# Strided attention scores that read ordered copies of q and k, made by Pool for each item

## The chip, the cores and the metric

The kernel runs on one core of one Trainium2 chip. The metric is the device time of one execution in microseconds; of several runs the median is taken. The core has five engines, each with an instruction list of its own that it takes in order: TensorE (PE; its weight loads are shown as PEld), VectorE (DVE), ScalarE (ACT), GpSimd (POOL) and SyncE (SP, which issues DMAs). They meet through semaphores.

## The reference

One layer of a hybrid decoder for a prompt of 2048 positions (and a small sample group of 8 x 4 rows), width 1024. What matters here is the attention of the prompt: 8 heads of 64 channels, each with three branches of dilated sliding windows, merged by the sums of their softmaxes:

```python
BRANCHES = ((128, 1), (512, 4), (2048, 16))      # window, dilation
def _dilated_prompt(q, k, v, bias_hj, d, nj):
    L = S // d
    ...
    s = jnp.einsum('bnqrhc,bnkrhc->bnrhqk', qb, kc).astype(jnp.float32)
    s = s * (HEAD_DIM ** -0.5) + bias[None, None, None]
    s = jnp.where(valid[None, :, None, None], s, NEG_INF)
    lse = jax.nn.logsumexp(s, axis=-1)
    p = jnp.exp(s - lse[..., None])
    o = jnp.einsum('bnrhqk,bnkrhc->bnqrhc', p.astype(vc.dtype), vc)
```

With dilation 16 a position sees only positions with the same residue modulo 16: each of the 16 residues is a causal attention of its own over 128 positions. Before the attention stand a normalisation and the input projection, behind it the output projection, a feed-forward network and a last normalisation.

## The kernel before

**Stages.** The input projection takes about the first 600 us, the attention the time from about 610 to 975 us, and output projection and feed-forward network the rest. The order on each engine is written out by hand: a planner (class `Plan`, lines 45 to 62) collects calls as (step, phase, function), and runs them step by step, within a step in the order of the phases "early", "exp", "low", "scores", "turn", "mid", "values", "out", "misc", "store". What a function issues goes to the ends of the engines' lists at that moment. Nothing holds an engine to its step: it goes on as soon as its next instruction has what it waits for.

**Attention items.** For one head, q and k lie in SBUF as [128, 2048] tiles with the positions along the row (load_head, L815). q comes as a rounded high part twice over ("qh") and a low part ("ql"), k as high and low part one above the other, so that one product with qh and one with ql make scores of full precision. A head has 16 band items (branches 1 and 2: 128 queries against up to 640 keys) and 4 strided items (branch 3: four residues each). The list OTHER (L1082) puts the strided items of a head at steps 2, 7, 12 and 17 of 20; head 0 has a list of its own (FIRST, strided items at 8, 11, 14 and 16 of 20), and so has head 7 (LAST: at 1, 3, 5 and 7 of 20).

**One strided item**, placed at step x (L1147 on):
- step x, "scores": strided_scores (L921). For each of four residues two products of 128x128 on TensorE. Stationary operand and moving operand are read straight from the head's tiles with a step of 16 elements, which is 64 bytes.
- step x + 1, "scores": strided_bias (L929). DVE adds the bias (L932) and takes the row minima (L934), Pool subtracts them (L935).
- steps x + 3 to x + 5: exp on ACT (L938), row sums on DVE (L942), four transposes on TensorE (L947), rounding on ACT (L950), low parts on DVE (L896).
- from step x + 6: strided_values (L953). Eight products of 128x128 (L958, L959), whose operands lie packed; then strided_out on ACT (L966), which writes its result with a step of 16 elements.

**Pool in this stage** has only the subtractions of L935 and the merges of the head before (merge, L1031): for each of four chunks three operations of 128x512 (L1036, L1038, L1040), one a step, at steps 11 to 22 behind that head's end, so that the last three stand in the first steps of the head after; they wait for factors that come by DMA. In the "scores" phase of a step a subtraction stands ahead of the merge of that step, which is in phase "store".

Scores land in PSUM tiles "ps_s", of which there are two (L79). A band item's scores (L859), transposes (L887) and values (L910) fill the rest of TensorE's list.

Of the kernel before, what the change touches and what calls it, by code (L numbers as in the profile page):

```python
# [11 lines left out]
F32R = mybir.dt.float32r  # L12
# [7 lines left out]
P = 128  # L20
T = 2048
NT = T // P
# [20 lines left out]
class Plan:  # L43
# [8 lines left out]
    def at(self, step, phase, fn, *args):  # L52
        self.events.append((step, self.PHASES.index(phase), self.n, fn, args))
        self.n += 1
# [10 lines left out]
def hymba_step(ctx: ExitStack, tc: tile.TileContext, A: dict, O: dict):  # L65
    nc = tc.nc
    sync, act, dve, pool, pe = nc.sync, nc.scalar, nc.vector, nc.gpsimd, nc.tensor
# [11 lines left out]
    def ps_s():  # L79
        return psum_s.tile([P, 2, 512], F32, name="ps_s", tag="s", bufs=2)  # L80
# [79 lines left out]
    at = plan.at  # L160
# [493 lines left out]
    for n in range(len(first) + 4):  # L654
        if n >= 4:
            (w_split if first[n - 4][0] == "w" else x_half_split)(*first[n - 4][1:])
        if n < len(first):
            if first[n][0] == "w":
                k = first[n][1]
# [39 lines left out]
    for half in range(2):  # L699
        for ki, kind in enumerate(ORDER[half]):  # L700
            for gi, tiles in enumerate(GROUPS):
                start = ((half * 5 + ki) * 3 + gi) * 8
                for k in range(KD):
                    if start == 0:

                        for j in range(3):
                            n = 3 * k + j
# [99 lines left out]
    heads, loads, sts, fs, obs, o3s = {}, {}, {}, {}, {}, {}  # L807
# [106 lines left out]
    def band_out(it):  # L914
# [3 lines left out]
        dst = obs[h][:, G * 512:(G + 1) * 512]  # L918
        act.activation(dst, it["grp"]["o"], AF.Copy)

    def strided_scores(it):  # L921
        d, st, r4 = it["d"], it["st"], it["n"]
        it["s"] = s = ps_s()[:, 0, :]
        for a in range(4):
            qs = bass.ds(r4 * 4 + a, P, step=NT)
            pe.matmul(s[:, a * P:(a + 1) * P], d["qh"][:, qs], d["k"][:, qs], start=True, stop=False)
            pe.matmul(s[:, a * P:(a + 1) * P], d["ql"][:, qs], d["k"][:, qs], start=False, stop=True)

    def strided_bias(it):  # L929
        d, st, r4, s = it["d"], it["st"], it["n"], it["s"]  # L930
# [155 lines left out]
    for h in range(H):  # L1086
        r4 = 0
# [31 lines left out]
    for h in range(H):  # L1119
# [4 lines left out]
        if end:  # L1124

            x = s0 - NI
# [21 lines left out]
    for i, it in enumerate(items):  # L1148
        x, h, n = B0 + i, it["h"], it["n"]

        at(x, "scores", scores, it)
        at(x + 1, "scores", bias, it)
        if it["kind"] == "s":
            at(x + 3, "exp", strided_exp, it)
            at(x + 4, "low", strided_sum, it)
            at(x + 4, "turn", strided_turn, it)
            at(x + 5, "mid", low_parts, it)
            v = min(y for y in range(x + 6, x + 14) if y not in taken)
            taken.add(v)
            at(v, "values", strided_values, it)  # L1160
            at(v + 1, "early", strided_out, it)
            continue
        at(x + 2, "exp", band_exp, it)
        at(x + 3, "turn", band_turn, it)
        at(x + 4, "low", low_parts, it)
        if n % 4 == 3:
            for part in range(3):
                at(x + 4 + part, "values", band_values, it, part)
            at(x + 7, "early", band_out, it)
# [9 lines left out]
    ap_ = left.enter_context(tc.tile_pool(name="attn", bufs=2, reuse_waits="tile"))  # L1179
# [525 lines left out]
    h = H - 1  # L1705
# [321 lines left out]
```

## Time and profile before

| what | value |
|---|---|
| median of 3 runs | 2704.91 us (2699.18 to 2713.04) |
| profiled execution | 2700.58 us, its span 2698.8 us |
| TensorE busy | 2554.9 us (95% of the span) |
| DVE, ACT, Pool busy | 1421.3, 1246.3, 1312.4 us |
| granted TensorE clock, mean | 0.966 |
| attention, 580 to 950 us: TensorE, DVE, ACT, Pool busy of 370 us | 339.9, 266.7, 255.0, 141.1 us |

A row of a group reads: line, engine, operation, result<-operands by the program's names, shape, count, then busy us, mean ns of one, and the idle time of the engine ahead of it with what ended that. A row of a timeline reads: start in us from the span's start, duration in us, engine, line, operation, count, and in brackets how long the engine sat idle before and on whom it waited. Matmuls are pipelined: one that starts every 0.11 us may be shown with 0.28 us each, so a pace is read from the starts of the weight loads.

### The profile page before, as it was taken

The page shows a single profiled execution, that of the slowest core. Times are in us where ns is not written, and L with a number is a line of the kernel's source. Part 1 is how long each engine was busy: PE and PEld are TensorE (multiplying, and loading weights), DVE is VectorE, ACT ScalarE, POOL GpSimd, SP SyncE. Part 2 cuts the span into 40 slices and gives each one's busy share as a digit, 9 for nine tenths or more (in the row PEclk, how much of TensorE's full clock was granted, in tenths as well). Part 3 has the DMA queues.
Part 4 walks back from the last instruction along what each step waited for, and adds up shares of the span by engine and source line. Part 5 has one row for each costly group of instructions (what it writes and reads, how often), then busy time and mean ns, then how long its engine had stood idle before and what let it go on. Part 6 is the DMA issues. An engine that isn't in the chain of part 4 may idle for free. (4 is left out here: it accounts for less than half of the span.)

```text
span 2698.8 us, 38876 instructions
## 1 busy us (share of the span) xinstructions
PE 2554.9 (95%) x13578; PEld 2253.8 (84%) x13578; DVE 1421.3 (53%) x2884; ACT 1246.3 (46%) x2649; POOL 1312.4 (49%) x960
## 2 busy tenths in 40 slices
PE   8998899998999978999999999999999998999997
PEld 6777677677888866999998987899999987999996
DVE  3268784436887864444434455344444455444445
ACT  5414344446777645645455444423232335433333
POOL 1036653221445353767676743536353533666663
PEclk9999899998999989899999999899999999899998
DMA  8765844686576565436455465436354553455553
GB/s 244 218 201 157 283 137 134 187 273 201 160 239 181 155 177 175 136 126 199 153 181 166 162 188 162 159 122 214 138 198 153 183 163 125 166 201 202 203 195 117
DMA packets 314679, 481.05 MB, mean 178 GB/s; under 512 B 26967, under 2 KB 179720, under 8 KB 308596
## 3 DMA queue, kind: packets, MB, share of 16 engines
q1 hardware_dynamic: 300100, 455.89, 52.1%
q10 hardware_dynamic: 14384, 22.68, 3.2%
q8 instruction: 108, 1.77, 0.3%
q14 instruction: 87, 0.71, 0.1%
HBM read 382.76 MB, written 165.84 MB: 203 GB/s over the span
## 5 line engine op out<-in xcount | busy, mean ns | idle before, releaser
L1472 POOL TENSOR_TENSOR op<-fr,op 128x512 fp32r<-128x512 f32 x385 | 489.0, 1299 | 318.3 <-ACT op L1468 281.1
L1529 PE MATMUL ps_m<-xh,op 128*128 128x384 f32 (+4 forms) x1932 | 629.6, 326 | 8.5 <-ACT xh L1406 5.3
L1530 PE MATMUL ps_m<-xl,op 128*128 128x384 f32 (+4 forms) x1932 | 627.8, 325 | 7.0 <-DVE xl L1409 7.0
L1531 PE MATMUL ps_m<-xh,op 128*128 128x384 f32 (+4 forms) x1932 | 627.6, 325 | 0.0
L1602 PE MATMUL ps_o<-dw,hw 128*128 128x512 f32 x2040 | 484.4, 392 | 8.8 <-DVE acc L1604 8.8
L1602 PEld LDWEIGHTS ps_o<-dw,hw 128*128 128x128 f32 x2040 | 379.6, 188 | 91.5 <-DVE acc L1604 15.9
L1529 PEld LDWEIGHTS ps_m<-xh,op 128*128 128x128 f32 x1932 | 377.6, 195 | 13.7 <-ACT xh L1406 5.9
L1530 PEld LDWEIGHTS ps_m<-xl,op 128*128 128x128 f32 x1932 | 377.8, 196 | 11.7 <-DVE xl L1409 7.7
L1531 PEld LDWEIGHTS ps_m<-xh,op 128*128 128x128 f32 x1932 | 377.3, 195 | 0.0
L1604 DVE TENSOR_TENSOR acc<-acc,ps_o 128x512 f32<-128x512 f32 (+1 forms) x362 | 247.0, 687 | 213.7 <-PE ps_o L1602 213.6
L1569 ACT ACTIVATE ps_t<-zn 128x384 f32<-128x384 f32 (+1 forms) x126 | 58.3, 463 | 481.1 <-DVE zn L1552 372.8
L1468 ACT ACTIVATE op<-fr 128x512 fp32r<-128x512 f32 x396 | 235.7, 622 | 19.0 <-DMA fr<-ab_d 13.7
L137 POOL TENSOR_TENSOR dw<-fd,dw 128x1024 fp32r<-128x1024 f32 x66 | 158.7, 2404 | 122.9 <-ACT dw L134 122.7
L317 PE MATMUL ps_s<-wh,xh 128*128 128x512 f32 x480 | 197.7, 412 | 6.7 <-ACT xh L134 6.7
L318 PE MATMUL ps_s<-wl,xh 128*128 128x512 f32 x480 | 192.2, 401 | 0.0
L319 PE MATMUL ps_s<-wh,xl 128*128 128x512 f32 x480 | 191.4, 399 | 0.0
L1472 POOL TENSOR_TENSOR op<-pair,op 128x512 fp32r<-128x512 f32 x63 | 81.3, 1299 | 116.1 <-ACT op L1468 116.1
L1579 ACT ACTIVATE hw<-ps_t 128x384 fp32r<-128x384 f32 (+1 forms) x126 | 56.1, 453 | 176.6 <-DVE ps_t L1575 175.6
L317 PEld LDWEIGHTS ps_s<-wh,xh 128*128 128x128 f32 x480 | 92.8, 193 | 36.5 <-issue 8.3
L935 POOL TENSOR_TENSOR e<-e,st 128x512 f32<-128x512 f32 x32 | 33.3, 1042 | 173.5 <-DVE st L934 118.1
L319 PEld LDWEIGHTS ps_s<-wh,xl 128*128 128x128 f32 x480 | 92.7, 193 | 20.6 <-DVE xl L137 0.2
L318 PEld LDWEIGHTS ps_s<-wl,xh 128*128 128x128 f32 x480 | 93.0, 194 | 18.4 <-DVE wl L225 1.1
(457 smaller groups left out, 4912.1 us busy)
## 6 DMA issues: line engine op xcount, KB each, us to landing
fr<-ab_d SPq DMA_DIRECT2D x308, 256.0 KB
fd<-in_w_down_dram SPq DMA_DIRECT2D x66, 512.0 KB
out_ks_dram<-in_cache_k_dram SPq DMA_DIRECT2D x56, 512.0 KB
out_vs_dram<-in_cache_v_dram SPq DMA_DIRECT2D x56, 512.0 KB
ab_d<-fr SPq DMA_DIRECT2D x88, 256.0 KB
raw<-in_w_in_dram SPq DMA_DIRECT2D x72, 256.0 KB
qk_d<-pair SPq DMA_DIRECT2D x64, 256.0 KB
ab_d<-pair SPq DMA_DIRECT2D x63, 256.0 KB
```

The lines of the kernel that those rows point to most:

```text
L137: (eng_lo or pool).tensor_sub(lo, src, hi.bitcast(F32))
L317: pe.matmul(o[j], xh[:, k, :], wh, start=(k == 0), stop=False)
L318: pe.matmul(o[j], xh[:, k, :], wl, start=False, stop=False)
L319: pe.matmul(o[j], xl[:, k, :], wh, start=False, stop=(k == KD - 1))
L1468: act.activation(ops[f, j][0], ab[f][j], AF.Copy)
L1472: (pool if f or j in POOL_LOW else dve).tensor_sub(lo_, ab[f][j], hi.bitcast(F32))
L1529: pe.matmul(out, wh[:, ks], xh[:, :, k], start=(k == 0), stop=False)
L1530: pe.matmul(out, wh[:, ks], xl[:, :, k], start=False, stop=False)
L1531: pe.matmul(out, wl[:, ks], xh[:, :, k], start=False, stop=(k == 3))
L1569: act.activation(g, c, AF.Silu)
L1602: pe.matmul(ps[0:nr], l_, r_[:, cs], start=(z == 0 and y == 0), stop=(z == FC - 1 and y == len(pairs) - 1))
L1604: dve.tensor_add(B.acc[i][0:nr, cs], B.acc[i][0:nr, cs], ps[0:nr])
```

## The change

A new function, strided_order, makes for each strided item a tile "sq" with three parts: k, qh and ql of that item's four residues, each residue's 128 positions packed. Pool makes it by three tensor_copy instructions, each of 128 x 4 x 128 elements, which read with a step of 16 elements and write packed. strided_scores reads its operands from that tile. There are two such tiles. The copies of an item at step x are put into the plan at step x - 2, phase "out". The products, their number, shapes and order stay the same, and so do all instructions of the other engines.

```diff
+    def strided_order(h, r4):
+
+        d = heads[h]
+        d["sq", r4] = t_ = ap_.tile([P, 3, 4, P], F32R, name="sq", tag="sq", bufs=2)
+        for z, nm in enumerate(("k", "qh", "ql")):
+            pool.tensor_copy(t_[:, z], d[nm].rearrange("p (i r) -> p r i", r=NT)[:, r4 * 4:r4 * 4 + 4])
+
     def strided_scores(it):
-        d, st, r4 = it["d"], it["st"], it["n"]
+        d, r4 = it["d"], it["n"]
         it["s"] = s = ps_s()[:, 0, :]
+        t_ = d.pop(("sq", r4))
         for a in range(4):
-            qs = bass.ds(r4 * 4 + a, P, step=NT)
-            pe.matmul(s[:, a * P:(a + 1) * P], d["qh"][:, qs], d["k"][:, qs], start=True, stop=False)
-            pe.matmul(s[:, a * P:(a + 1) * P], d["ql"][:, qs], d["k"][:, qs], start=False, stop=True)
+            for z in (1, 2):
+                pe.matmul(s[:, a * P:(a + 1) * P], t_[:, z, a], t_[:, 0, a], start=(z == 1), stop=(z == 2))
...
         if it["kind"] == "s":
+            at(x - 2, "out", strided_order, h, n)
             at(x + 3, "exp", strided_exp, it)
```

## The prediction, made before the changed kernel ran

> **What bounds the kernel now.** I read the page first, then the busy times by stretches, the groups by line and shape for the attention stage (600 to 945 us), and last the timelines of TensorE's weight loads and of Pool. The page gives the span, the table of stretches one head of the attention (head 3):
>
> ```profile
> span 2698.8 us, 38876 instructions
> core 0: us, PE busy (x) PEld busy (x) DVE busy (x) ACT busy (x) POOL busy (x), PEclk, DMA share, GB/s
> 747.00:789.00 42.00, 40.09 (x263) 36.45 (x264) 34.59 (x87) 32.22 (x77) 18.69 (x16) 1.00 0.66 209
> ```
>
> TensorE is busy 40.09 of 42 us, so a head is as long as TensorE's list, plus what TensorE has to wait. DVE (34.59) and ACT (32.22) are close behind. Pool has 23.3 us to spare, but room in the sum says nothing about when it is free. The groups and the weight loads around item 2 of that head show what the change is after:
>
> ```profile
> L926 PEld LDWEIGHTS ps_s<-k,qh 128*128 128x128 f32 x128 | 39.4, 307 | 1.5 <-DVE st L865 0.9 <-PE ps_o L910 0.6
> L958 PEld LDWEIGHTS ps_o<-eh,v 128*128 128x128 f32 x120 | 23.6, 196 | 0.6 <-ACT ob L919 0.6
> ```
>
> ```profile
> 766.40 0.19 PEld L958 LDWEIGHTS ps_o<-eh,v 128*128 128x128 f32 x1
> ...
> 767.18 0.19 PEld L959 LDWEIGHTS ps_o<-el,v 128*128 128x128 f32 x1
> 767.29 0.30 PEld L926 LDWEIGHTS ps_s<-k,qh 128*128 128x128 f32 x1
> ...
> 768.80 0.31 PEld L927 LDWEIGHTS ps_s<-k,ql 128*128 128x128 f32 x1
> 769.52 0.20 PEld L887 LDWEIGHTS ps_o<-ident,e 128*128 128x128 f32 x2 [0.41 <-ACT e L870]
> ```
>
> L958 and L959 are the strided value products: the same 128x128 shape as the strided scores of L926 and L927, but from operands that lie side by side. Eight of them start between 766.40 and 767.18, one each 0.111 us. The eight score products, whose columns lie 64 bytes apart, start between 767.29 and 768.80, one each 0.216 us.
>
> **Part 1, TensorE's saving.** From the ordered copy a score product should go at the pace of L958: 8 x (0.216 - 0.111) = 0.84 us an item, and 32 items give 26.9 us. All of it lies on TensorE's own list. It can be less: in the last row above TensorE waits right behind the scores for an exp on ACT, and there a faster score product only lengthens the wait. I take the whole 26.9 us, and keep the doubt for the range.
>
> **Part 2, the price of a copy.** Each item adds three Pool copies of 128x512, 96 in all, and no DMA. The trace has no Pool copy and no strided read on Pool, so I bound the price by these rows:
>
> ```profile
> L935 POOL TENSOR_TENSOR e<-e,st 128x512 f32<-128x512 f32 x32 | 33.3, 1042 | 173.5 <-DVE st L934 118.1
> masks.py:199 POOL TENSOR_SCALAR_AFFINE_SELECT ident<-ident 128x128 f32<-128x128 f32 x1 | 0.3, 295 | 0.1
> masks.py:197 POOL MEMSET ident<- 128x128 f32 x1 | 0.2, 205 | 0.3 <-POOLq L2013 0.3
> L2013 POOL MEMSET const-float32-1.0<- 128x1 f32 x1 | 0.1, 99 | 0.0
> L1183 DVE TENSOR_REDUCE sel_g<-ident x1: 269/269/269, 598.4 to 598.4; 128x8 f32<-128x128 f32 x1
> L1184 DVE TENSOR_REDUCE sel_r<-ident x1: 355/355/355, 598.6 to 598.6; 128x16 f32<-128x128 f32 x1
> L919 ACT ACTIVATE ob<-ps_o 128x512 f32<-128x512 f32 x28 | 16.6, 594 | 3.9 <-PE ps_o L910 3.6
> L966 ACT ACTIVATE o<-ps_o 128x512 f32<-128x512 f32 x30 | 31.5, 1051 | 5.5 <-PE ps_o L959 2.6
> ```
>
> The only Pool operation with one input (the affine select) takes 295 ns for 128 columns; 99 ns is what an instruction on one column takes. So 196 ns go into 128 columns, and 512 columns packed would take 0.10 + 4 x 0.196 = 0.88 us. For the 64-byte step there are three witnesses on other engines, each with its packed twin: ACT's write (L966 against L919) costs 0.46 us more for 512 columns, TensorE's weight load (L926 against L958) 0.11 for 128, so 0.44 for 512, and DVE's read (L1184 against L1183) 0.086 for 128, so 0.34 for 512. Two of the three say 0.45: I take 0.88 + 0.46, about **1.35 us** a copy, 4.05 us for the three. The bounds: 0.52 us, if a copy goes at the memset's pace (0.10 + 4 x 0.106) and the step is free; and 1.84 us, if it costs what L935 with its two inputs costs and suffers ACT's ratio, 1.042 x 1051/594. [...]
>
> **Part 3, where the copies stand.** Pool takes its list in order. The copies for the item at step x are put at step x - 2, behind what stands there. With strided items at steps 2, 7, 12 and 17 of a head, the list is: subtraction (L935) of item 0, copies 1, subtraction 1, copies 2, two merge operations, subtraction 2, two merges, copies 3, three merges, subtraction 3, two merges, copies for the next head's item 0, three merges. So every set of copies stands right behind the subtraction of the item before it, and that subtraction waits for a DVE reduction of scores which TensorE has only just made. This is a new ring: scores of one item, DVE, subtraction, perhaps two merges, copies, scores of the next item. The room that it has is the time from the end of the subtraction to the next scores, head 3 again:
>
> ```profile
> 752.08 1.04 POOL L935 TENSOR_TENSOR e<-e,st 128x512 f32<-128x512 f32 x1 [2.95 <-DVE s L993]
> 761.82 1.04 POOL L935 TENSOR_TENSOR e<-e,st 128x512 f32<-128x512 f32 x1 [8.70 <-DVE st L934]
> ...
> 772.99 1.04 POOL L935 TENSOR_TENSOR e<-e,st 128x512 f32<-128x512 f32 x1 [1.61 <-DVE st L934]
> 773.98 1.30 POOL L1040 TENSOR_TENSOR ob<-ob,o 128x512 f32<-128x512 f32 x1
> 775.24 1.29 POOL L1036 TENSOR_TENSOR ob<-ob,pair 128x512 f32<-128x512 f32 x1
> ...
> 784.20 1.04 POOL L935 TENSOR_TENSOR e<-e,st 128x512 f32<-128x512 f32 x1 [3.83 <-PE ps_s L859]
> ```
>
> ```profile
> 756.68 0.30 PEld L926 LDWEIGHTS ps_s<-k,qh 128*128 128x128 f32 x1
> 778.49 0.30 PEld L926 LDWEIGHTS ps_s<-k,qh 128*128 128x128 f32 x1
> 789.33 0.30 PEld L926 LDWEIGHTS ps_s<-k,qh 128*128 128x128 f32 x1
> ```
>
> ```profile
> 772.15 0.69 DVE L934 TENSOR_REDUCE st<-e 128x4 f32<-128x512 f32 x1
> ```
>
> The scores start at 756.68, 767.29, 778.49 and 789.33. The room is 3.56, 4.43, 4.46 and 4.09 us. It stays the same when the scores get 0.84 us shorter, because the subtraction then comes as much earlier. Needed are 4.05 us for the copies and 0.15 for handing over (the reduction ends at 772.84, the subtraction behind it starts at 772.99): 4.2 us in the first two gaps. In the last two the two merges (1.30 + 1.29) stand in between, so 6.8 us. What is missing is a stall of TensorE: 0.64, 0, 2.34 and 2.71, together **5.7 us a head** against 3.4 us saved. I count heads 1 to 5 like this (28.5 us), and head 6 without its last gap (3.0).
>
> The first and the last head have their items closer together:
>
> ```profile
> 620.11 1.04 POOL L935 TENSOR_TENSOR e<-e,st 128x512 f32<-128x512 f32 x1 [9.82 <-DVE st L934]
> 913.88 1.04 POOL L935 TENSOR_TENSOR e<-e,st 128x512 f32<-128x512 f32 x1 [3.80 <-DVE st L934]
> 922.76 1.04 POOL L935 TENSOR_TENSOR e<-e,st 128x512 f32<-128x512 f32 x1 [2.76 <-DVE st L934]
> ```
>
> ```profile
> 621.55 0.30 PEld L926 LDWEIGHTS ps_s<-k,qh 128*128 128x128 f32 x1 [0.87 <-DVE st L865]
> 916.89 0.30 PEld L926 LDWEIGHTS ps_s<-k,qh 128*128 128x128 f32 x1 [0.58 <-PE ps_o L910]
> 923.80 0.29 PEld L926 LDWEIGHTS ps_s<-k,qh 128*128 128x128 f32 x1
> 929.07 0.30 PEld L926 LDWEIGHTS ps_s<-k,qh 128*128 128x128 f32 x1
> 933.96 0.30 PEld L926 LDWEIGHTS ps_s<-k,qh 128*128 128x128 f32 x1
> ```
>
> In head 0 the copies of item 1 stand behind the subtraction that ends at 621.15, 0.40 us before the scores: 3.8 us of stall; its later copies have room. In head 7, item 0 has 1.97 us of room (914.92 to 916.89) and needs one merge and the copies, 5.5: 3.5 us. Item 1 needs two merges and the copies, 6.8 us, from the scores of item 0 on, and these now have 6.9 - 0.84: 0.7 us. Item 2 needs merge, subtraction, merge and copies, 7.8 us, and has 5.27 - 0.84: 3.4 us. Item 3 needs subtraction and copies, 5.2, and has 4.89 - 0.84: 1.2 us. Head 7 stalls 8.8 us.
>
> **The sum.** Stalls 28.5 + 3.0 + 3.8 + 8.8 = 44.1 us; saved 26.9 us; net **+17 us**. Against the profiled execution's own 2700.58 us that is 2718. The median of the runs shown, 2704.91, lies 4.3 us above it, and I forecast for a median: **2722 us**. Behind the attention everything moves by the same amount, since the next stage starts on the last head's result. Nothing waits for the three copies' reading but the two buffers of the copy itself, whose scores are two items old by then, and the head's tiles, which band products later on the same list hold longer anyway. Merges pushed back by some 4 us feed SP's stores of the heads, which are read only behind the attention; head 6's come after the last copies. I price them at nothing.
>
> **Rivals.**
> A, faster: the copies cost 0.52 to 0.88 us each. At 0.88 the same gaps give 18.7 us of stall, so -8 us (2697); at 0.52 only 4.3, so -23 us (2682). For it: Pool's memset pace. Against: its one-input row at 1.53 ns a column, and three witnesses that a 64-byte step is not free. [...] This is the side opposite to my forecast; it decides from a copy of about 1.1 us down, where stalls and savings cancel.
> B, a draw: a copy of 0.88 + 0.34 = 1.23 us, DVE's surcharge for its read in place of ACT's. The stalls are then 36 us and the sum is +9 us: 2714. Against it, two witnesses to one; for it, that DVE's is the only strided read into a vector engine. [...]
> C, far slower: Pool becomes the bound. It has 42 - 18.69 = 23.3 us a head for 12 copies, so from 1.94 us a copy its sum decides and not the ring. At my upper bound, 1.84, the ring gives 85 us of stall, +58 us (2763).
> D, the change doesn't do what it says: the slow pace of L926 comes from something else than the step. Then nothing is saved: +44 us (2749). Same shape, same engine and a pace of one half next to it speak against.
>
> **How the numbers follow.** This kernel's measurement tells about 0.5%, 13.5 us, from no change. Forecast (copies of 1.3 to 1.8 us, +13.5 to +57): 0.55. C: 0.05. D: 0.02. B and what lies within 13.5 us of it on both sides of nothing: 0.26. A beyond that: 0.12. So slower 0.62, same 0.26, faster 0.12. The range reaches from 2694 (A at 0.88 us, a little below) to 2765 (the upper bound).
>
> **What would show it.** The copies' mean on Pool (1.35 expected). Score products one each 0.11 us, loads near 196 ns. New rows of TensorE waiting for Pool ahead of the score products, near 44 us in the attention, longest in head 7 and ahead of items 3 and 0, none ahead of item 2. Pool near 35 of 42 us in a head. I am wrong if TensorE's wait for Pool stays under 20 us, if the loads keep their 307 ns, or if DVE's chain shortens after a stall and gives the room back.

## The result, and the profile after the change

| kernel | median of runs | profiled execution |
|---|---|---|
| before | 2703.51 us (2699.18 to 2713.04, 4 runs) | 2700.58 us |
| changed | 2725.19 us (2722.42 to 2727.54, 4 runs) | 2722.42 us |

The changed kernel is slower: ratio 1.0083, 95% interval 1.0059 to 1.0107, which is +22 us (16 to 29). The forecast was 2722 us. The total is close, but two of its three terms are far off and a fourth is missing, as the profile begins to show. First the head of the page of the changed kernel (span, then busy time, share and instructions of each engine):

```profile
span 2720.6 us, 39008 instructions
PE 2543.6 (93%) x13578; PEld 2240.0 (82%) x13578; DVE 1444.1 (53%) x2884; ACT 1247.2 (46%) x2649; POOL 1408.5 (52%) x1056
```

Pool's busy time grew by 96.1 us, from 1312.4 to 1408.5, for its 96 copies. But DVE's grew too, by 22.8 us from 1421.3, and the change does not touch one instruction of DVE. That is the first sign of what the forecast left out. Line by line, 18.7 us of the growth lie in six operations of the attention's statistics (two of their rows follow below), and 3.6 us in L225 of the input projection, beside which no copy runs.

The table of stretches, one head of the attention (the same head 3, which now lies at 753 to 801 us), and the whole attention:

```profile
core 0: us, PE busy (x) PEld busy (x) DVE busy (x) ACT busy (x) POOL busy (x), PEclk, DMA share, GB/s
753.00:801.00 48.00, 41.42 (x267) 38.54 (x266) 37.91 (x89) 33.02 (x79) 31.84 (x29) 0.89 0.63 188
600.00:985.00 385.00, 321.52 (x2078) 290.88 (x2077) 291.47 (x669) 257.31 (x606) 237.15 (x212) 0.92 0.61 177
```

The head takes 48 us where it took 42; TensorE now idles 6.6 us of it instead of 1.9. Part of the growth is the granted clock, 0.89 in this head and 1.00 before: TensorE is busy 41.42 us where it was 40.09, although its score products got shorter. Pool has 16 us to spare in the sum, and still TensorE waits for it. The weight loads of the four strided items of that head (start, duration, engine, line, count, in brackets the idle time before and its releaser):

```profile
753.42 0.19 PEld L934 LDWEIGHTS ps_s<-sq 128*128 128x128 f32 x1 [0.53 <-POOL sq L926]
754.42 0.86 PEld L934 LDWEIGHTS ps_s<-sq 128*128 128x128 f32 x7 [0.81 <-POOL sq L926]
767.05 1.83 PEld L934 LDWEIGHTS ps_s<-sq 128*128 128x128 f32 x8
778.51 0.97 PEld L934 LDWEIGHTS ps_s<-sq 128*128 128x128 f32 x8
789.85 0.19 PEld L934 LDWEIGHTS ps_s<-sq 128*128 128x128 f32 x1
790.85 0.86 PEld L934 LDWEIGHTS ps_s<-sq 128*128 128x128 f32 x7 [0.81 <-POOL sq L926]
```

Two forecasts can be read here. The pace is as foretold: eight loads in 0.97 us, the last of them 0.19 long, so starts 0.111 us apart. (The 1.83 us of item 1 lies in a stretch, 766 to 772 us, in which the granted clock was 0.50.) The ring shows where it was expected, ahead of items 0 and 3, behind two merges, and not ahead of item 2; nor is there a wait ahead of item 1, where 0.64 us was forecast. But it is short: the first product starts as soon as k and qh are there, and only the other seven loads wait for the copy of ql. The waits of the attention stage (who waited for whom: us in total, times, longest), changed kernel:

```profile
PE ps_s L859 <- DVE st L865: 17.6, 23, 1.8
PEld ps_s L934 <- POOL sq L926: 16.6, 20, 2.5
```

and of the kernel before, the row that answers to the first, and two that are needed further down:

```profile
PE ps_s L859 <- DVE st L865: 9.9, 21, 2.1
PE ps_t L887 <- DVE el L896: 7.9, 11, 3.1
PE ps_o L887 <- DVE el L896: 4.8, 6, 2.3
```

TensorE's wait for Pool is 16.6 us, not 44. Beside it TensorE waits longer for DVE: its band scores (L859) wait 17.6 us instead of 9.9 until DVE has read an earlier tile of scores (L865).

**Why DVE is late.** The timelines of Pool and of DVE in head 3 of the changed kernel, side by side:

```profile
760.00 1.08 POOL L926 CAST sq<-k 128x512 fp32r<-128x512 f32 x1
761.02 1.07 POOL L926 CAST sq<-qh 128x512 fp32r<-128x512 f32 x1
762.03 1.03 POOL L926 CAST sq<-ql 128x512 fp32r<-128x512 f32 x1
```

```profile
760.14 0.97 DVE L1006 TENSOR_TENSOR f<-s,st 128x16 f32<-128x16 f32 x1
761.14 0.97 DVE L1007 TENSOR_TENSOR f<-f,s 128x16 f32<-128x16 f32 x1
762.04 1.05 DVE L1008 TENSOR_TENSOR f<-f,st 128x16 f32<-128x16 f32 x1
```

These three small operations of the softmax statistics (class Stats; lines 999 to 1001 of the kernel before) work on 16 columns. Each now lasts about 1 us, and each ends within 0.03 us of the copy beside it: 761.11 and 761.08, 762.11 and 762.09, 763.09 and 763.06. Two lines of the statistics with all their operations, before (count, then ns min/median/max, first and last start):

```profile
L983 DVE TENSOR_TENSOR sm<-st,sel_g x9: 415/1020/1435, 658.0 to 976.0; 128x256 f32<-128x256 f32 x8, 128x128 f32<-128x128 f32 x1
L1001 DVE TENSOR_TENSOR f<-f,st x9: 160/167/1033, 665.1 to 983.2; 128x16 f32<-128x16 f32 x8, 64x16 f32<-64x16 f32 x1
```

and after, where the lines have moved by seven:

```profile
L990 DVE TENSOR_TENSOR sm<-st,sel_g x9: 415/1424/6577, 662.3 to 1001.8; 128x256 f32<-128x256 f32 x8, 128x128 f32<-128x128 f32 x1
L1008 DVE TENSOR_TENSOR f<-f,st x9: 157/1033/1057, 669.5 to 1008.9; 128x16 f32<-128x16 f32 x8, 64x16 f32<-64x16 f32 x1
```

The shortest stay what they were (0.16 us for L1008); its median goes from 0.17 to 1.03 us, that of L990 from 1.02 to 1.42, and one of L990 lasts 6.58 us. What these operations have in common is that both operands lie in SBUF. The rows of L896, with one operand in PSUM, do not change: with 384 columns they took 554 ns, and still do, with 256 columns 414 and 413. The last row's last start also shows what the attention lost: 1008.9 instead of 983.2 us, 25.7 us.

The trace of the kernel before already had this to show. DVE in its head 3, and the first two weight loads of its strided items 0 and 1:

```profile
752.59 0.56 DVE L999 TENSOR_TENSOR f<-s,st 128x16 f32<-128x16 f32 x1
```

```profile
746.76 0.30 PEld L926 LDWEIGHTS ps_s<-k,qh 128*128 128x128 f32 x1
...
756.68 0.30 PEld L926 LDWEIGHTS ps_s<-k,qh 128*128 128x128 f32 x1
```

and, of the changed kernel, the weight load that comes behind the three held operations:

```profile
764.08 0.30 PEld L859 LDWEIGHTS ps_s<-k,qh 128*128 128x128 f32 x2 [1.99 <-DVE st L865]
```

L999 ends at 753.15; Pool's subtraction in the prediction's row (752.08, 1.04 us) ends at 753.12. The shortest instance of L999 takes 0.16 us. One subtraction of 1.04 us could hold one of these operations; three copies behind each other hold all three. Where the statistics stand, between items 0 and 1, the head grew most: from 746.76 to 756.68 it was 9.9 us, from 753.42 to 767.05 it is 13.6. The wait of 1.99 us behind the held operations is about half of these 3.7 us. The other half is the granted clock, which was 0.50 from 756 to 758 us and again from 766 us: the same TensorE work took 3.92 us in place of 2.85 (755.22 to 759.14 us, before 748.59 to 751.44) and, behind the wait, 2.97 in place of 2.25.

The 6.58 us in head 7, first DVE, then Pool at that time:

```profile
943.98 6.58 DVE L990 TENSOR_TENSOR sm<-st,sel_g 128x256 f32<-128x256 f32 x1
```

```profile
943.82 1.30 POOL L1045 TENSOR_TENSOR o<-o,pair 128x512 f32<-128x512 f32 x1
945.05 1.07 POOL L942 TENSOR_TENSOR e<-e,st 128x512 f32<-128x512 f32 x1
946.05 1.29 POOL L1047 TENSOR_TENSOR ob<-ob,o 128x512 f32<-128x512 f32 x1
947.26 1.05 POOL L926 CAST sq<-k 128x512 fp32r<-128x512 f32 x1
948.24 1.06 POOL L926 CAST sq<-qh 128x512 fp32r<-128x512 f32 x1
949.21 1.05 POOL L926 CAST sq<-ql 128x512 fp32r<-128x512 f32 x1
```

DVE's operation starts inside the first of six Pool instructions that follow each other without a gap, and ends at 950.56, 0.3 us after the last of them (950.26). An operation of 0.4 us stood until Pool stopped.

The rows above show this much: operations of 0.16 to 0.17 us last 0.97 to 1.05 us and end with the copy beside them. The row of L999 before (0.56 us, ending with the subtraction) spoke against the change, and the prediction passed over it. By the rows the wait can also outlast one Pool instruction: six of them went by. What holds the operations no row shows.

So the theory after the profile: **the price of the copies is in good part DVE's, held while Pool copies, and not only TensorE's wait for Pool.** The rival is the prediction's own: the ring sets the time, and the held operations have room. The expectations below call the theory "the port"; that is a name for the holds, and no run shows more of it.

### The profile page after: what moved, and what is told of

Same layout as the page of the kernel before. It is cut to its first block, busy times and chain, and to the rows that moved or that the text cites. A ratio compares the mean times of both kernels' runs of the same rounds, so it can differ in the third digit from the quotient of the medians.

```text
span 2720.6 us, 39008 instructions
## 1 busy us (share of the span) xinstructions
PE 2543.6 (93%) x13578; PEld 2240.0 (82%) x13578; DVE 1444.1 (53%) x2884; ACT 1247.2 (46%) x2649; POOL 1408.5 (52%) x1056
## 5 line engine op out<-in xcount | busy, mean ns | idle before, releaser
L1476 ACT ACTIVATE op<-fr 128x512 fp32r<-128x512 f32 x396 | 235.6, 622 | 18.2 <-DMA fr<-ab_d 16.3
L1448 ACT ACTIVATE fr<-fr,g2c 128x128 f32<-128x128 f32 x352 | 107.4, 389 | 0.2 <-DMA fr<-in_w_up_dram 0.2
```

The lines of the kernel that those rows point to most:

```text
L1448: act.activation(w_[:, k * P:(k + 1) * P], w_[:, k * P:(k + 1) * P], AF.Copy, scale=g2c[:, kk:kk + 1])
L1476: act.activation(ops[f, j][0], ab[f][j], AF.Copy)
```

## The experiments

Each ratio is to the kernel before on the same chip, with its 95% interval.

**1 and 2. Saving alone, copies alone.** The kernel before with the scores read from packed columns (other positions than the right ones), without copies; and the changed kernel with its copies, whose scores read the head's tiles as before.

```diff
--- before
+++ packed_nocopy
-            qs = bass.ds(r4 * 4 + a, P, step=NT)
+            qs = slice((r4 * 4 + a) * P, (r4 * 4 + a + 1) * P)
--- changed
+++ copies_unused
...
-            for z in (1, 2):
-                pe.matmul(s[:, a * P:(a + 1) * P], t_[:, z, a], t_[:, 0, a], start=(z == 1), stop=(z == 2))
+            qs = bass.ds(r4 * 4 + a, P, step=NT)
+            pe.matmul(s[:, a * P:(a + 1) * P], d["qh"][:, qs], d["k"][:, qs], start=True, stop=False)
+            pe.matmul(s[:, a * P:(a + 1) * P], d["ql"][:, qs], d["k"][:, qs], start=False, stop=True)
```

> The kernel before, but its strided scores read 128 columns that lie side by side in the head's tiles instead of every sixteenth; no copies, so the scores are of the wrong positions. It gives what the packed reading is worth by itself. If all of the saving lands on the end of the list: 27 us faster than before (ratio 0.990), score products one each 0.111 us. If DVE's and ACT's chains hold TensorE back where it gets ahead: 10 to 18 us faster, and the rest of the 27 us is found as new waiting of TensorE for DVE and ACT.

> The changed kernel with its copies on Pool, but the scores read the head's tiles with the step as before; nobody reads the copies. Theory 1 (the ring: the loss is TensorE's wait for the copies): no wait, so the time of before, within 5 us. Theory 2 (the port: DVE's small operations with both operands in SBUF are held until a Pool copy ends, about 18 us more on DVE): 10 to 20 us slower than before, with the same longer operations on DVE as in the changed kernel and no wait for Pool.

Measured: packed_nocopy 0.9977 (0.9954 to 0.9999), 6 us less, of which the interval allows 0 to 12; even the lower of the two expectations was 10 to 18. The 26.9 us that TensorE's list got shorter did not come out as time. Waits of the attention, packed_nocopy:

```profile
PE ps_t L887 <- DVE el L896: 21.3, 18, 3.1
PE ps_o L887 <- DVE el L896: 10.6, 9, 2.3
```

The two waits for the low parts (L896) were 7.9 and 4.8 us before and are 21.3 and 10.6 here. TensorE arrives earlier and waits for the low parts, which DVE makes no sooner. copies_unused: 1.0061 (1.0043 to 1.0080), +16 us (12 to 22), although nothing reads the copies and TensorE waits for none. Its held operations and its wait for DVE, the latter to be set beside 9.9 us before:

```profile
L1008 DVE TENSOR_TENSOR f<-f,st x9: 158/1052/1077, 667.4 to 1003.9; 128x16 f32<-128x16 f32 x8, 64x16 f32<-64x16 f32 x1
```

```profile
PE ps_s L859 <- DVE st L865: 18.7, 26, 1.8
```

Copies without any ring cost most of what the whole change costs. The rival would have had this kernel level with the one before.

**3. The price of a copy.** The copies read packed columns (other positions), all else as changed.

```diff
-            pool.tensor_copy(t_[:, z], d[nm].rearrange("p (i r) -> p r i", r=NT)[:, r4 * 4:r4 * 4 + 4])
+            pool.tensor_copy(t_[:, z], d[nm].rearrange("p (r i) -> p r i", r=NT)[:, r4 * 4:r4 * 4 + 4])
```

> The changed kernel, but Pool copies columns that lie side by side (wrong positions), so its read has no step of 64 bytes. If the step costs what my price said: a copy goes from 1.08 to about 0.6 us, Pool's copies in all from 103 to 60 us, TensorE's wait for them from 17 us to under 5. If the step is free on Pool: 1.08 us again and the time of the changed kernel within 5 us. The DVE operations that are held by copies get shorter with the copies.

Measured: 1.0016 (0.9999 to 1.0033), +4 us. The copies of the changed kernel and of this one:

```profile
L926 POOL CAST sq<-k x32: 1052/1078/1123, 612.6 to 956.3; 128x512 fp32r<-128x512 f32 x32
```

```profile
L926 POOL CAST sq<-k x32: 607/612/630, 617.0 to 940.2; 128x512 fp32r<-128x512 f32 x32
```

The 64-byte step costs 0.46 us a copy, exactly the surcharge that the prediction took from ACT. The packed base is 0.62 us, not 0.88. Copies of 0.62 us in place of 1.08 give back about 18 of the 22 us; TensorE's wait for Pool falls to 3.3 us, and the median of L1008 to 632 ns from 1033. Both theories shrink together here, so this run settles the price and not the cause.

**4. The ring alone taken away.** In heads 1 to 6 the copies stand three steps earlier on Pool's list, so that they no longer follow the subtraction that waits for the scores just before.

```diff
-            at(x - 2, "out", strided_order, h, n)
+            at(x - (5 if 0 < h < H - 1 else 2), "out", strided_order, h, n)
```

> The changed kernel, but in heads 1 to 6 the copies of an item are put five steps ahead of it instead of two, so ahead of the subtraction of the item before: the ring is open, and the copies have a whole interval of items for themselves. Theory 1 (the ring): TensorE's wait for the copies in heads 1 to 6 (about 10 of 17 us) goes, and the time falls by that to 8 to 14 us above before. Theory 2 (the port): the time moves with how many of DVE's small operations still fall into copies; if as many as now, the sum of their durations stays 18 us above that of before and the kernel stays 10 us or more slower than before.

Measured: 1.0073 (1.0046 to 1.0100), as the changed kernel. Waits, early:

```profile
PE ps_t L887 <- DVE el L896: 23.3, 18, 3.1
PE ps_s L859 <- DVE st L865: 18.3, 23, 1.8
PEld ps_s L934 <- POOL sq L926: 5.0, 4, 2.5
```

The wait for Pool goes from 16.6 to 5.0 us, and the time does not move: TensorE waits for DVE instead, and L859 waits for DVE as long as in the changed kernel. So the ring is there, but taking it away by itself is worth nothing that can be measured: 3 us less than the changed kernel, and the two intervals together allow from 7 more to 13 less, so that a gain of the 12 us that TensorE waits less for Pool is not excluded by this run alone.

**5 and 6. The held operations taken away.** In heads 1 to 6 the statistics are left out, and the factors of head 0 are stored in their place; once in the kernel before, once in the changed one.

```diff
+    kept = []
     def stats_of(h, steps, r0, r1):
+        if 0 < h < H - 1:
+            def again():
+                kept[0].h = h
+                kept[0].store()
+            at(*steps[5], again)
+            return
...
+        if h == 0:
+            at(*steps[0], lambda: kept.append(d["s"]))
```

> The kernel before, but heads 1 to 6 do no statistics of their own (DVE's small operations with both operands in SBUF, their two small products, the exp): they store the factors of head 0 once more. It is the base for the next run; a few us faster than before, since DVE has about 2.5 us less to do in each of six heads.

> The changed kernel with the same work left out as in before_nostats, so that in heads 1 to 6 DVE has no operation left that a Pool copy could hold. Theory 2 (the port) alone: against before_nostats it is 0 to 6 us faster, like the packed reading without copies. Port and ring together: the ring's waits (about 17 us, less what the packed reading saves) are left, 4 to 12 us slower than before_nostats. If neither the port nor those operations matter (the clock, or the ring alone): still 20 us slower than before_nostats.

Measured: before_nostats 0.9998 (0.9981 to 1.0016), after_nostats 1.0018 (0.9992 to 1.0044). The same 96 copies now cost about 5 us (-2 to 12 against the kernel before) instead of 22, and the statistics by themselves cost the kernel before nothing. Against before_nostats it is 5 us too (-3 to 14): what was expected of holds and ring together, though the interval also holds what was expected of the holds alone. after_nostats, waits and busy times:

```profile
PEld ps_s L934 <- POOL sq L926: 15.9, 18, 2.5
PE ps_s L859 <- DVE st L865: 10.4, 20, 1.9
```

```profile
PE 2533.4 (94%) x13554; PEld 2230.5 (83%) x13554; DVE 1406.7 (52%) x2824; ACT 1246.8 (46%) x2643; POOL 1407.0 (52%) x1056
```

The wait for Pool is the changed kernel's (15.9 against 16.6), so the ring is untouched; what is gone is the wait of L859 (10.4 us) and DVE's surplus: 1406.7 us busy, beside this in before_nostats:

```profile
PE 2559.4 (95%) x13554; PEld 2258.8 (84%) x13554; DVE 1407.0 (52%) x2824; ACT 1246.0 (46%) x2643; POOL 1311.2 (49%) x960
```

Pool has the changed kernel's 96 us more, and DVE nothing more. This is the main evidence for the theory: copies beside DVE's statistics are dear, copies beside none are cheap. One reservation: without the statistics DVE also has more room to catch up, which by itself may soften any wait.

**7 and 8. Which operand.** Only k is copied (32 copies), or only qh and ql (64 copies); the other operand is read with its step.

```diff
--- changed
+++ k_only
...
-                pe.matmul(s[:, a * P:(a + 1) * P], t_[:, z, a], t_[:, 0, a], start=(z == 1), stop=(z == 2))
+                pe.matmul(s[:, a * P:(a + 1) * P], d[q][:, qs], t_[:, 0, a], start=(z == 1), stop=(z == 2))
--- changed
+++ q_only
...
-                pe.matmul(s[:, a * P:(a + 1) * P], t_[:, z, a], t_[:, 0, a], start=(z == 1), stop=(z == 2))
+                pe.matmul(s[:, a * P:(a + 1) * P], t_[:, z, a], d["k"][:, qs], start=(z == 1), stop=(z == 2))
```

> The changed kernel with only k copied (32 copies of 96): the moving operand is packed, the weights are still read with the step. Pace of the score products: 0.11 us if the moving operand alone sets it, 0.216 if the weight load does, about 0.16 if each pays for itself. A third of the copies holds DVE for a third of the time: by the port theory 4 to 8 us slower than before less what the pace brings (up to 3 us); the ring is open, with no wait for Pool.

> The changed kernel with only qh and ql copied (64 copies of 96): the weights are packed, the moving operand is still read with the step. Pace: the counterpart of k_only (0.216 if the moving operand alone sets it, 0.11 if the weight load does). Port theory: 8 to 14 us slower than before, wait for Pool under 8 us.

Measured: k_only 1.0033 (1.0008 to 1.0058), q_only 1.0064 (1.0034 to 1.0093), so +9 and +17 us. The first and the last of eight weight loads, k_only, then all eight, q_only:

```profile
771.72 0.30 PEld L937 LDWEIGHTS ps_s<-sq,qh 128*128 128x128 f32 x1
...
773.24 0.31 PEld L937 LDWEIGHTS ps_s<-sq,ql 128*128 128x128 f32 x1
```

```profile
772.47 0.97 PEld L937 LDWEIGHTS ps_s<-k,sq 128*128 128x128 f32 x8
```

With only the moving operand packed the pace stays (773.24 - 771.72) / 7 = 0.217 us; with only the stationary one packed it is the full 0.11. In these two runs the weight load alone sets it, and the copy of k buys nothing: a third of the copies was for no gain. All the same q_only stays slow, with two thirds of the copies and the whole gain in pace.

**9 to 12. Lighter statistics.** The mask product (L983) goes to Pool; the difference of the minima is read from PSUM; the exponents come from two operations with one tensor each. Only four small operations with two SBUF operands are left on DVE. Tried in the kernel before, in the changed one, with the early copies, and with early copies of qh and ql alone.

```diff
-            dve.tensor_tensor(self.m, self.st["t"][:, 0:2, 0:n].unsqueeze(3).broadcast_to([P, 2, n, 8]),
+            pool.tensor_tensor(self.m, self.st["t"][:, 0:2, 0:n].unsqueeze(3).broadcast_to([P, 2, n, 8]),
...
-            dve.tensor_tensor(f[:, 2, :], self.s[:, 0, :], m3, op=OP.min)
-            dve.tensor_sub(f[:, 0, :], f[:, 2, :], self.s[:, 0, :])
-            dve.tensor_sub(f[:, 1, :], f[:, 2, :], m3)
+            dve.tensor_scalar(f[:, 0, :], f[:, 2, :], -1.0, 0.0, op0=OP.mult, op1=OP.min)
+            dve.tensor_scalar(f[:, 1, :], f[:, 2, :], 0.0, None, op0=OP.min)
```

> The kernel before with its statistics rewritten to the same result: the mask product of a head (128x256) goes to Pool, the difference of the two minima is read from PSUM where it stands, and the two exponents come from it by operations with one tensor. DVE keeps only the four tiny operations of the weights that read two tensors in SBUF. Base of the next three; within 3 us of before, or up to 5 faster, since merges of Pool held these operations already here.

> The changed kernel with the statistics of before_light: all 96 copies, the ring as it is, but hardly anything on DVE that a copy can hold. Port theory: of the 22 us that the change costs, 13 to 19 go, so 3 to 9 us slower than before. If the port is not the cause: still 18 us or more slower.

> after_light with the copies of heads 1 to 6 put five steps ahead, so that the ring is open too. If the ring's waits cost what the profile shows for them, it gains 5 to 10 us on after_light and ends at 3 us faster to 3 us slower than before. If DVE's and ACT's chains set the pace as soon as TensorE gets ahead, it stays level with after_light, and the wait for Pool turns up as wait for DVE.

> early_light with only qh and ql copied (the weights; the moving operand k is read with the step, which costs TensorE nothing by the run that copied these two alone). It has a third less on Pool and should be the best with copies: level with the packed reading without copies, 3 to 8 us faster than before, if ring and port were the only costs. If it is not faster than before, a cost is left that neither explains.

Measured: before_light 1.0012 (0.9999 to 1.0024); after_light 1.0073 (1.0059 to 1.0088); early_light 1.0081 (1.0064 to 1.0098); q_early_light 1.0004 (0.9993 to 1.0016). after_light missed its expectation: beside before_light it still loses 16 us (1.0073 against 1.0012). Waits, and one of the operations that were left, after_light, then the same operation in before_light:

```profile
PEld ps_s L934 <- POOL sq L926: 15.5, 19, 2.5
PE ps_s L859 <- DVE st L865: 9.9, 20, 1.5
```

```profile
L1015 DVE TENSOR_TENSOR dd<-f,st x9: 159/1075/1096, 668.4 to 998.3; 128x16 f32<-128x16 f32 x8, 64x16 f32<-64x16 f32 x1
```

```profile
L1008 DVE TENSOR_TENSOR dd<-f,st x9: 158/163/171, 664.9 to 988.9; 128x16 f32<-128x16 f32 x8, 64x16 f32<-64x16 f32 x1
```

The hold moved on to the next operation of its kind (0.16 to 1.08 us), though the wait of L859 is down to 9.9 us, the kernel before's. The ring's wait stays (15.5). That these two together kept the time is argued, not shown. early_light has both below the changed kernel's (the wait for Pool is 6.0 us, that of L859 13.7, against 16.6 and 17.6), and is not faster either; there even an operation with one tensor in SBUF lasts up to 3.69 us, against 0.16 us at its shortest (the execution traced is the longest of six, 2736.77 us):

```profile
L1007 DVE TENSOR_SCALAR f<-f x9: 164/402/3686, 669.9 to 1006.7; 128x16 f32<-128x16 f32 x8, 64x16 f32<-64x16 f32 x1
```

Without copies the same operation (L1000 in before_light) has a median of 466 ns and 598 at its longest. That Pool holds it too is an inference from these times; no row shown sets it beside a Pool instruction. Why early_light is not faster was not found. q_early_light, with a third of the copies gone as well, is level with the kernel before and some 21 us below the changed one. It was expected to beat the kernel before by 3 to 8 us and does not. That the 32 copies of k are worth 21 us between these last two runs is more than any price measured here explains. No version with copies on Pool that was run beats reading with the step.

## Why the prediction was right in the sum and wrong in its terms

- **Part 1, the saving: the pace right, its worth wrong.** 0.11 us a load came as forecast. "I take the whole 26.9 us" failed: alone it is worth 6 us (0 to 12), because TensorE then waits for DVE and ACT: 21.3 + 10.6 us for the low parts where it waited 7.9 + 4.8, and its weight loads 16.3 + 6.1 us for an exp on ACT (L870) where they waited 7.5 + 1.9. The sentence ahead of it named this ("a faster score product only lengthens the wait"), and the sum left it out.
- **Part 2, the price of a copy: over-sized.** 1.08 us (median of L926), not 1.35. The step's surcharge, 0.46, was right; the base, scaled from the affine select, was 0.26 too high. With 1.08 us one is at the prediction's own crossing point ("about 1.1 us"): with the true price its sum would have forecast no change.
- **Part 3, the ring: the place right, its size wrong.** It stands ahead of items 0 and 3, and not ahead of item 2. It is 16.6 us, not 44.1: the copies are shorter, and the first product waits for two of the three. That is under the 20 us below which the prediction called itself wrong. In head 7, for which it had 8.8 us, TensorE waits only ahead of item 0 (0.95 and 0.81 us); the longest single wait, 2.46 us, is that of head 0, for which it had 3.8. Taken away (early) it gives nothing back that could be measured.
- **The term that was missing.** "Nothing waits for the three copies' reading but the two buffers of the copy itself" failed. DVE's statistics wait for it: their six operations are busy 18.7 us longer with the same work, copies that nobody reads cost 16 us, and the whole change costs 5 us where the statistics are left out.
- **The sum.** +17 was forecast as 44.1 less 26.9. Measured are 16 for the copies beside DVE, less 6 for the faster scores, and 22 in all, so some 12 are left for the ring and for what the parts do to each other. The three intervals, put together in quadrature, leave that term open by about 10 us either way. The near hit is luck: it came from a stall put some 27 us too high (44.1 against a wait of 16.6) and a saving put 21 us too high (26.9 against 6), which largely cancel, and from a term that was missing.
- **Rivals.** A's price (0.52 to 0.88 us) was not met, C is out (Pool has 16 us of a head to spare), D is out (the step does set the pace). B's price was nearer than the forecast's own, and its +9 was too little for the same missing term.

**What stays open.** Ring and holds don't add up as separate prices. Without the ring the time stays (early); with the largest holds gone it nearly stays (after_light); with the statistics gone it falls by 17 us although the ring is there (after_nostats); and early_light, which should have lost both, does not fall. That either one suffices to keep TensorE late is argued from these four, not shown. The granted clock is a rival that is only half settled: the attention of the changed kernel has 0.92 (in the table of stretches above) and that of the kernel before 0.96, but after_nostats has 0.92 as well and loses 5 us:

```profile
600.00:985.00 385.00, 327.47 (x2128) 294.54 (x2127) 274.38 (x647) 269.18 (x632) 251.21 (x224) 0.92 0.60 179
```

so it does not decide by itself. Its share can be estimated from the single executions. In 77 of the kernel before, on three chips, the mean clock lies between 0.958 and 0.971 and the time between 2718 and 2688 us; a straight line through them falls by 2.1 us for each 0.001. The four of the changed kernel have 0.9605 in the mean, the 77 have 0.9653. By that line some 10 of the 22 us go with the lower clock, and the changed kernel still lies 13 us above it. copies_unused lies 10 us above the line, before_nostats and after_nostats 3 and 5 us below. So the copies' price beside the statistics does not come from the clock alone; why the clock is lower, and whether that is a cause of the delay or follows from it, stays open.

## What to carry to other kernels

Before work goes to an engine with room to spare, list which operations the other engines do at that time, and where their operands lie: here DVE operations with both operands in SBUF stood until the Pool instructions beside them ended (the median of L1008 went from 0.17 to 1.03 us), and the profile shows it as a longer operation, not as a wait. A faster TensorE step is worth only what the engines ahead of it let through (here 6 of 26.9 us), so take the saving alone in a run before counting it. A total that comes out right proves none of its terms: each needs its own row or its own run.

## What the runs showed of the hardware that was not expected

- In the rows shown, DVE operations with two SBUF operands last until the Pool instruction beside them ends (0.17 us became 1.03), and up to 6.58 us over six Pool instructions without a gap. An operation with one SBUF tensor, tensor_scalar, was seen at 3.69 us in early_light, against 0.16 us at its shortest. L896, with one operand in PSUM, did not change (554 ns both times).
- The pace of the 128x128 score products followed the step of the stationary operand alone: 0.217 us each with a step of 64 bytes (k_only), 0.11 packed; with the moving operand read at that step (q_only) it was 0.11, as with both packed (the changed kernel).
- A Pool copy of 128x512 took 0.62 us packed (packed_source) and 1.08 us with a 64-byte read step (the changed kernel), 1.75 times as long.
